# A retention block on one Trainium2 core: head outputs turned by four VectorE instructions a head, with the blocks put in place through DRAM

## The chip, the cores and the metric

The kernel runs on one core of one Trainium2 chip. Times are microseconds of device time. Matrix products run on TensorE (PE), elementwise work on VectorE (DVE) and ScalarE (ACT), small work and the software DMA queue on GpSimd (POOL), the hardware DMA queue on SyncE (SP). Each engine executes its own list of instructions strictly in order; semaphores join the lists. An instruction that waits holds everything behind it on its engine.

## The reference

One encoder layer on 512 tokens of width 1024, in float32:

```python
h = rmsnorm(x, g_mix);  proj = h @ w_in          # xc, gb, gc, q, k, v, g_sw, gate_a, gate_r
y_a = (gb * dwconv3(gc * xc)) @ w_a_out
ret = Ret_fwd(q, k, v) + Ret_bwd(q, k, v)        # 4 heads, q/k 256 wide, v 512 wide, rotary on q and k
ret = (ret - mean) * rsqrt(var + 1e-6)           # per token and head, over the 512 values
y_r = (ret * g_ret * silu(g_sw)) @ w_r_out       # 2048 x 1024
x = x + (sigmoid(gate_a) * y_a + sigmoid(gate_r) * y_r) @ w_o
x = x + (silu(h2 @ w_gate) * (h2 @ w_up)) @ w_down,  h2 = rmsnorm(x, g_ffn);  y = rmsnorm(x, g_final)
```

## The kernel before, in words

Every float32 operand is split into a high part in float32r and a low rest (`split`, L200: the high part on ACT at L203 or L206, the low part on DVE at L204 or L207), and each product is three matmuls, high by high, high by low, low by high (`mm3`, L340). Large products use a Strassen form (`strassen`, `fm_quad`). Weights come in pieces of 512 KB on the SP queue into a pool of 10 `raw` buffers, and are split into 5 pairs `whi`/`wlo` that are reused in turn.

The program first makes all projections. What is needed later is kept in DRAM: v and the silu of the gate, `sgd`, for each of the four heads (`do_quad`, L745, stores by `store`, L632, on the POOL queue), rotated q and k (`keep`), gates for the merge. Then comes the stage of the heads (L942 to L974):

- `load_head` brings q, k, v and the gate of the next head to SBUF on the SP queue.
- `do_scores` makes the 512 x 512 table of scores of a head, times its decay, 128 source tokens at a time (24 matmuls), and splits it into `p`.
- `do_pv` multiplies by v. For each tile `nb` of 128 tokens, 12 matmuls fill one PSUM bank with 128 tokens x 512 values; DVE takes mean and variance (L894 to L896), POOL the power (L897), DVE subtracts the mean and multiplies by the gate (L903), ACT scales (L905). The result lies in `sg`, tokens on partitions. At the last tile of a head, `sum_step` puts up to four DRAM transfers on the POOL queue (`t_o`), which add weight quarters for a later stage.
- `do_t` (L907) turns it: `transpose` (L212) issues 16 DVE instructions a head, each moving one quarter of 32 partitions to another, so that features lie on partitions. Then four `split`s with the gain `g_ret` make `yr`.
- `do_wr` multiplies `yr` by 512 rows of `w_r_out`, in two halves of 512 columns, each with four PSUM banks (96 matmuls in all), and adds to `ysum` (ACT copies at L935 for head 0, DVE adds at L937 for the others).

On PE the stage runs pv(0), scores(1), `do_mix(3)`, pv(1), scores(2), wr(0), pv(2), scores(3), wr(1), pv(3), wr(2), wr(3). So head h is turned after pv(h), and `yr` is first read one product later; for head 3 only wr(2) lies between. There are 8 PSUM banks (`psum`, L180) used in turn. A scheduler sets the order of each engine's list: it interleaves the instructions by its own forecast, and the order is then fixed.

Of the kernel before, what the change touches and what calls it, by code (L numbers as in the profile page):

```python
# [14 lines left out]
AF = mybir.ActivationFunctionType  # L15
ALU = mybir.AluOpType

P = 128
# [3 lines left out]
NB = S // P  # L22
HEADS = 4
# [148 lines left out]
def block_kernel(ctx: ExitStack, tc: tile.TileContext, xw0, xw, xT, xtok, wpack, wquad, cols, decs, rot, g_ffn, g_final, out):  # L172
    nc = tc.nc
# [26 lines left out]
    def split(src, hi, lo, scale=None, round=None):  # L200

        if scale is None:
            first = (round or nc.scalar.copy)(hi, src)  # L203
            low_of[0] = nc.vector.tensor_tensor(out=lo, in0=src, in1=hi.bitcast(F32), op=ALU.subtract)  # L204
        else:
            first = nc.scalar.activation(hi, src, AF.Copy, scale=scale)  # L206
            nc.vector.scalar_tensor_tensor(  # L207
                out=lo, in0=src, scalar=scale, in1=hi.bitcast(F32),
                op0=ALU.mult, op1=ALU.subtract)
        return first  # L210

    def transpose(out, src):  # L212

        for b in range(4):
            for q in range(4):
                i = src[32 * b:32 * b + 32].rearrange("p j (i q c) -> p j i q c", q=4, c=32)
                o = out[32 * q:32 * q + 32].rearrange("p i (j b c) -> p j i b c", b=4, c=32)
                nc.vector.transpose(o[:, :, :, b, :], i[:, :, :, q, :])


    pos = [0]
    block = [0]
# [42 lines left out]
    def sum_step(behind, among="quads"):  # L265

        if steps[among]:
            quad, f, g, u, add = steps[among].pop(0)
            src = wsum[quad, g, u] if g[0] == "t" else quarter(quad, g, u)
            with tc.issue_after(behind.ins):  # L270
                if add:
                    nc.gpsimd.dma_start(out=wsum[quad, f, u], in_=src, accum_op=ALU.add, max_dma_last_dim=4 * CH)
                else:
                    nc.gpsimd.dma_start(wsum[quad, f, u], src)
# [65 lines left out]
    def mm3(ps, left, right, first, last):  # L340
        (lh, ll), (rh, rl) = left, right
        nc.tensor.matmul(ps, lh, rh, start=first, stop=False)  # L342
        nc.tensor.matmul(ps, lh, rl, start=False, stop=False)  # L343
        nc.tensor.matmul(ps, ll, rh, start=False, stop=last)  # L344

    def act_pair(tiles, k, sl=slice(0, S)):
        hi, lo = tiles
        return hi[k // 4][:, k % 4, sl], lo[k // 4][:, k % 4, sl]
# [7 lines left out]
                mm3(ps, c.w(k, m * P, P), act_pair(rhs, k), k == 0, k == 7)  # L356
            evict(block0 + m, ps)

    def token_major(lhs, row0, chunks, evict, before=None):


        pss = [bank() for _ in range(NB)]
        n = 4 * chunks
        for kk in range(n):
            if kk % 4 == 0:
                c = Chunk()
            if before:
                before(kk)
# [117 lines left out]
    gret = cols_sb[:, O_GRET:O_GRET + 16]  # L486
# [109 lines left out]
    def decays():  # L596
        d = []
        for base, op in ((0, ALU.max), (-384, ALU.min)):
            delta = t512(mybir.dt.int32)
            nc.gpsimd.iota(delta, pattern=[[1, 512]], base=base, channel_multiplier=-1)  # L600
            d.append(t512())
            nc.vector.tensor_scalar(out=d[-1], in0=delta, scalar1=0.0, scalar2=None, op0=op)
        for h in range(HEADS):
            f, g = t512(), t512()
            nc.scalar.activation(f, d[0], AF.Exp, scale=lgam[:, h:h + 1])
            nc.scalar.activation(g, d[1], AF.Exp, scale=lgam[:, 4 + h:5 + h])
            nc.vector.tensor_tensor(out=f[:, 0:P], in0=f[:, 0:P], in1=g[:, 384:512], op=ALU.mult)
            store(tabs[h][:, 0:384], g[:, 0:384])
            store(tabs[h][:, 384:896], f)
# [3 lines left out]
    def kept(name):  # L613
        return dram.tile([P, 4, 512], F32, name=name)
# [17 lines left out]
    def store(dst, t):  # L632
        return nc.gpsimd.dma_start(dst, t)
# [4 lines left out]
    for h in range(EARLY):  # L638
        pss = [bank() for _ in range(4)]
        for kk in range(8):  # L640
            if kk % 4 == 0:
                c = Chunk()
# [23 lines left out]
        t = bigtile()  # L666
# [77 lines left out]

    def do_quad(left, right, func, func_left=None):  # L745
        def ev_sum(dst, o, f):
            def ev(tt, t):
                if f:
                    nc.scalar.activation(t, t, f)
                last = store(dst[:, o + tt, :], t)  # L750
                if tt and not o:
                    sum_step(last)
            return ev

        def ev21(tt, ps):
            t = t512()
            nc.scalar.activation(t, ps, func_left or AF.Copy)
            last = store(left[:, 2 + tt, :], t)
            if tt:
                turn_one()  # L760
                sum_step(last)
        strassen(4, xforms, ev_sum(left, 0, func_left), ev21, ev_sum(right, 2, func), ev_sum(right, 0, func))

    decays()
    for h in range(HEADS):
        do_quad(vd[h], sgd[h], AF.Silu)
        if h >= EARLY:
            do_qk(h)
    for j in range(2):
        do_quad(gad[j], grd[j], AF.Sigmoid, AF.Sigmoid)  # L770
    while held:
        turn_one()

# [89 lines left out]
    def do_scores(qk, tab):  # L863
        p = (bigtile(F32R), bigtile(F32R))
        for mb in range(NB):
            ps = bank()
            for d in range(2):
                sl = slice(mb * P, (mb + 1) * P)
                mm3(ps, (qk[0][:, 2 + d, sl], qk[1][:, 2 + d, sl]), (qk[0][:, d, :], qk[1][:, d, :]),
                    d == 0, d == 1)  # L870
            t = t512()
            o = (3 - mb) * P
            nc.vector.scalar_tensor_tensor(out=t, in0=ps, scalar=QK ** -0.5, in1=tab[:, o:o + 512],
                                           op0=ALU.mult, op1=ALU.mult)
            split(t, p[0][:, mb, :], p[1][:, mb, :])
        return p

    def split_v(v):
# [48 lines left out]
    def do_wr(h, yr):  # L927

        if h == 0:
            ysum.extend([bigtile(), bigtile()])  # L930
        for half in range(2):
            def ev(nb, ps):
                t = ysum[half][:, nb, :]
                if h == 0:
                    nc.scalar.copy(t, ps)  # L935
                else:
                    nc.vector.tensor_tensor(out=t, in0=ps, in1=t, op=ALU.add)  # L937
                if h == HEADS - 1:
                    nc.vector.tensor_tensor(out=t, in0=t, in1=sgr[half][:, nb, :], op=ALU.mult)
            token_major(yr, 0, 1, ev)  # L940

    mix_quads()  # L942
    nxt = load_head(0)
    p = do_scores(nxt[0], nxt[1])
    vv, sg = split_v(nxt[2]), nxt[3]
    do_mix(2)
    yr = None
    for h in range(HEADS):
# [5 lines left out]
        t = sg  # L954
        if h < HEADS - 1:
            p = do_scores(nxt[0], nxt[1])
# [10 lines left out]
        yr = new  # L967
# [107 lines left out]
    a, d, b = po["a"], [bank(), bank()], [bank(), bank()]  # L1075
# [227 lines left out]
    a, d, b = ([bank(), bank()] for _ in range(3))  # L1303
# [120 lines left out]
```

## Time and profile before

| what | value |
|---|---|
| median of 3 runs | 1022.72 us (1022.34 to 1023.39) |
| profiled execution, first to last instruction | 1021.7 us |
| PE busy | 1013.2 us (99%) |
| PE weight loads | 883.2 us (86%) |
| DVE busy | 902.5 us (88%) |
| ACT busy | 548.4 us (54%) |
| POOL busy | 151.7 us (15%) |
| HBM read and written | 162.8 MB and 57.4 MB |

The profile lists the profiled execution by its span alone; the three timed runs lie 0.6 to 1.7 us above that span. In the profile a line `L218` is a line of the source, the arrow `out<-in` names what an instruction writes and reads, and a square bracket in the timeline tells how long the engine had been idle before the instruction and what ended the wait. DMA landing times run from the issue to the arrival of the data.

### The profile page before, as it was taken

The numbers are of one execution on the slowest core, as the hardware profiler recorded it, in microseconds if no ns is written. First come the engines' busy times: TensorE is split into PE (matmuls) and PEld (weight loads), VectorE is DVE, ScalarE is ACT, GpSimd is POOL, SyncE is SP. The second block draws the span as 40 slices with busy tenths as digits, with TensorE's granted clock in tenths as the row PEclk, the third lists the DMA queues.
The fourth block names the chain that finished last, engine by engine and source line by source line (L and its number), as shares of the span: only waits on it lengthen the run. The fifth ranks groups of instructions, "written<-read, shape, count | busy, mean of one in ns | idle before, by whom it ended". The sixth has DMA issues, their size and how long they took to land.

```text
span 1021.7 us, 14821 instructions
## 1 busy us (share of the span) xinstructions
PE 1013.2 (99%) x5586; PEld 883.2 (86%) x5586; DVE 902.5 (88%) x1161; ACT 548.4 (54%) x744; POOL 151.7 (15%) x238
## 2 busy tenths in 40 slices
PE   9999999999999999999999999999999999999997
PEld 7888888888888998888888888889998999899986
DVE  7878998979798888797989997999898999889996
ACT  7547665553655455343543325586654565556554
POOL 0030221222122003202122100020001410110011
PEclk9999999999999999999999999999999999999999
DMA  9525587695767657839597855484316562663523
GB/s 354 188 81 185 173 296 212 214 310 162 249 196 238 250 203 268 333 130 349 124 331 294 272 200 169 157 264 132 107 42 242 172 154 83 198 153 104 165 69 98
DMA packets 53992, 202.34 MB, mean 198 GB/s; under 512 B 7392, under 2 KB 7520, under 8 KB 49312
## 3 DMA queue, kind: packets, MB, share of 16 engines
q1 hardware_dynamic: 37600, 137.39, 39.0%
q0 software_dynamic: 16032, 63.71, 21.3%
q8 instruction: 44, 0.72, 0.3%
q10 hardware_dynamic: 288, 0.29, 0.1%
q14 instruction: 28, 0.23, 0.1%
HBM read 162.82 MB, written 57.41 MB: 216 GB/s over the span
## 4 chain that ended last, share of the span: by engine, by line
PE 98%; DVE 1%; ACT 0%; issue 0%; POOL 0%; POOLq 0%; ACTq 0%
PE bank L427 39%; PE bank L383 27%; PE bank L342 10%; PE bank L343 10%; PE bank L344 10%; PE bank L477 0%; PE bank L1053 0%; PE bank L998 0%; PE bank L662 0%; DVE raw L301 0%; DVE big L1296 0%; ACT whi L203 0%; DVE wlo L204 0%; POOL fin L1286 0%; POOL ac L1035 0%
## 5 line engine op out<-in xcount | busy, mean ns | idle before, releaser
L203 ACT CAST whi<-raw 128x1024 fp32r<-128x1024 f32 (+2 forms) x299 | 302.8, 1028 | 265.0 <-PE bank L427 67.1
L204 DVE TENSOR_TENSOR wlo<-raw,whi 128x1024 fp32r<-128x1024 f32 (+2 forms) x300 | 352.7, 1192 | 68.0 <-ACT whi L203 67.7
L383 PE MATMUL bank<-xform,whi 128*128 128x256 f32 x1424 | 258.2, 284 | 0.3 <-ACT whi L203 0.3
L383 PEld LDWEIGHTS bank<-xform,whi 128*128 128x128 f32 x1424 | 222.3, 192 | 2.0 <-ACT t L434 0.8
L383 PE MATMUL bank<-xform,wlo 128*128 128x256 f32 x712 | 200.7, 283 | 0.0
L427 PE MATMUL bank<-whi,big 128*128 128x512 f32 x596 | 187.0, 389 | 0.0
L427 PE MATMUL bank<-whi,xform 128*128 128x512 f32 x496 | 157.1, 390 | 0.0
L301 DVE TENSOR_TENSOR raw<-raw 128x1024 f32<-128x1024 f32 (+1 forms) x128 | 152.0, 1203 | 4.2 <-DMA raw<-wquad 3.3
L383 PEld LDWEIGHTS bank<-xform,wlo 128*128 128x128 f32 x712 | 136.4, 192 | 0.0
L427 PEld LDWEIGHTS bank<-whi,big 128*128 128x128 f32 x596 | 111.9, 188 | 23.8 <-ACT t L434 0.4
L427 PE MATMUL bank<-wlo,big 128*128 128x512 f32 x298 | 115.7, 389 | 0.0
L427 PEld LDWEIGHTS bank<-whi,xform 128*128 128x128 f32 x496 | 93.0, 188 | 19.7 <-DVE xform L204 0.6
L427 PE MATMUL bank<-wlo,xform 128*128 128x512 f32 x248 | 96.5, 389 | 0.0
L434 ACT COPY t<-bank 128x512 f32<-128x512 f32 x105 | 61.0, 587 | 56.3 <-PE bank L383 30.1
L342 PE MATMUL bank<-big,whi 128*128 128x512 f32 x220 | 85.7, 390 | 0.0
L344 PE MATMUL bank<-big,wlo 128*128 128x512 f32 x220 | 85.6, 389 | 0.0
L343 PE MATMUL bank<-big,whi 128*128 128x512 f32 x220 | 85.6, 389 | 0.0
L427 PEld LDWEIGHTS bank<-wlo,big 128*128 128x128 f32 x298 | 56.0, 188 | 11.4
L427 PEld LDWEIGHTS bank<-wlo,xform 128*128 128x128 f32 x248 | 46.6, 188 | 9.6
L342 PE MATMUL bank<-whi,big 128*128 128x512 f32 x128 | 49.8, 389 | 0.0
L343 PE MATMUL bank<-wlo,big 128*128 128x512 f32 x128 | 49.8, 389 | 0.0
L344 PE MATMUL bank<-whi,big 128*128 128x512 f32 x128 | 49.8, 389 | 0.0
(203 smaller groups left out, 1385.8 us busy)
## 6 DMA issues: line engine op xcount, KB each, us to landing
raw<-wquad SPq DMA_DIRECT2D x140, 512.0 KB, 4.7
raw<-wpack SPq DMA_DIRECT2D x42, 512.0 KB, 6.3
t_f<-wquad POOLq DMA_DIRECT2D x12, 512.0 KB, 8.0
z<-t POOLq DMA_DIRECT2D x24, 256.0 KB, 4.5
t_o<-wquad POOLq DMA_DIRECT2D x12, 512.0 KB, 6.7
zform<-z POOLq DMA_DIRECT2D x6, 1024.0 KB, 7.8
v<-t POOLq DMA_DIRECT2D x16, 256.0 KB, 5.7
sg<-t POOLq DMA_DIRECT2D x16, 256.0 KB, 4.8
```

The costliest lines, as they stand in the source:

```text
L203: first = (round or nc.scalar.copy)(hi, src)
L204: low_of[0] = nc.vector.tensor_tensor(out=lo, in0=src, in1=hi.bitcast(F32), op=ALU.subtract)
L301: nc.vector.tensor_tensor(out=t, in0=t, in1=raws[quad, more, u][:, 0:n], op=ALU.add)
L342: nc.tensor.matmul(ps, lh, rh, start=first, stop=False)
L343: nc.tensor.matmul(ps, lh, rl, start=False, stop=False)
L344: nc.tensor.matmul(ps, ll, rh, start=False, stop=last)
L383: nc.tensor.matmul(o, l[:, c], r[:, k], start=start and s == 0 and k == 0 and i == 0, stop=stop and k == 3 and i == 2, skip_group_check=True)
L427: nc.tensor.matmul(pss[tt], l, r[:, c], start=start and k == 0 and i == 0, stop=stop and k == n - 1 and i == 2, skip_group_check=True)
L434: nc.scalar.copy(t, ps)
```

## The change

`transpose` now issues four DVE instructions a head, one for each token tile `j`, over all 128 partitions. Each turns blocks of 32 x 32 inside every quarter of 32 partitions and writes them in runs of 32 into a tile `t`. The blocks then go from one quarter of the partitions to another through DRAM: four stores on the POOL queue (256 KB each, by `store`) put them into a DRAM tensor `turned[h]`, and one load of 1 MB on the SP queue brings it back.

Tokens are assigned to tiles in another way: tile `j`, partition 32 b + r is token 128 b + 32 j + r. The split of the scores (L204 and L203 on `t`) writes its columns in that order, and the gate of a head is stored by quarters of 32 rows (`by_quarter`). The splits after turning read and write 4 runs of 128 for each partition instead of one run of 512. `token_major` loses arguments that were not used. The products are the same.

```diff
-    def transpose(out, src):
-
-        for b in range(4):
-            for q in range(4):
-                i = src[32 * b:32 * b + 32].rearrange("p j (i q c) -> p j i q c", q=4, c=32)
-                o = out[32 * q:32 * q + 32].rearrange("p i (j b c) -> p j i b c", b=4, c=32)
-                nc.vector.transpose(o[:, :, :, b, :], i[:, :, :, q, :])
+    def transpose(h, out, src):
+
+        t = bigtile()
+        for j in range(NB):
+            o = t.rearrange("p q (i j r) -> p i q j r", i=4, j=4)[:, :, :, j, :]
+            nc.vector.transpose(o, src[:, j, :].rearrange("p (i q c) -> p i q c", i=4, q=4))
+        for q in range(4):
+            store(turned[h][32 * q:32 * q + 32].rearrange("c b f -> b c f"), t[:, q, :])
+        nc.sync.dma_start(out, turned[h])
...
-    def token_major(lhs, row0, chunks, evict, before=None):
+    def token_major(lhs, evict):
...
-                mm3(pss[nb], act_pair(lhs, row0 + kk, slice(nb * P, (nb + 1) * P)),
-                    c.w(kk % 4, 0, 512), kk == 0, kk == n - 1)
+                mm3(pss[nb], tuple(x[:, nb, kk * P:(kk + 1) * P] for x in lhs), c.w(kk, 0, 512), kk == 0, kk == 3)
...
+    turned = [kept(f"turned{h}") for h in range(HEADS)]
...
-                last = store(dst[:, o + tt, :], t)
+                last = store(dst(o + tt), t)
...
+    def by_quarter(d):
+        return lambda n: d[32 * n:32 * n + 32].rearrange("r j e -> j r e")
...
-        do_quad(vd[h], sgd[h], AF.Silu)
+        do_quad(by_tile(vd[h]), by_quarter(sgd[h]), AF.Silu)
...
-            split(t, p[0][:, mb, :], p[1][:, mb, :])
+            split(t.rearrange("p (b j r) -> p b j r", b=4, j=4),
+                  *(x[:, mb, :].rearrange("p (j b r) -> p b j r", b=4, j=4) for x in p))
...
     def do_t(h, t):
         tt = bigtile()
-        transpose(tt, t)
+        transpose(h, tt, t)
         yr = (bigtile(F32R), bigtile(F32R))
         for eb in range(4):
-            split(tt[:, eb, :], yr[0][:, eb, :], yr[1][:, eb, :], gret[:, 4 * h + eb:4 * h + eb + 1])
-        return [yr[0]], [yr[1]]
+            split(*(x[:, :, P * eb:P * eb + P] for x in (tt, *yr)), gret[:, 4 * h + eb:4 * h + eb + 1])
+        return yr
```

The lists of the engines move with it. Line numbers of the changed kernel are 3 or 4 higher in this stage: L939 there is L935 here, L941 is L937, L630 is L633, L858 is L855.

**ACT, head 1 turned while wr(0) runs.** `L203 big<-t` is the end of the split of the scores of head 2, `L206` the high half of the split of the turned head 1, `L935` empties the banks of wr(0). Before:

```order
L203 CAST big<-t_4403 128x512
L203 CAST whi<-raw 128x1024 x2
L206 ACTIVATE big<-big,cols_sb 128x512 x4
L935 COPY big<-bank 128x512 x4
L203 CAST whi<-raw 128x1024
L935 COPY big<-bank 128x512 x4
```

And with the change:

```order
L203 CAST big<-t_4401 128x4x4x32
L203 CAST whi<-raw 128x1024 x3
L206 ACTIVATE big<-big,cols_sb 128x4x128 x4
L939 COPY big<-bank 128x512 x8
L203 CAST whi<-raw 128x1024
```

One cast of a weight moved ahead of the splits of head 1; all eight copies out of PSUM still stand behind them.

**POOL, head 3.** `L897` is the power of a token tile of pv(3), `L274` and `L272` copy and add weight quarters in DRAM, `L921` loads operands of the merge. Before:

```order
L897 TENSOR_TENSOR bnmv<-bnmv,mhalf 128x1
L274 DMA t_0_o<-t_0_o 16x8192
L274 DMA t_2_o<-t_2_o 16x8192
L272 DMA t_0_o<-wquad 64x2048
L272 DMA t_2_o<-wquad 64x2048
L921 DMA zform<-z_249 128x1024
```

And with the change:

```order
L901 TENSOR_TENSOR bnmv<-bnmv,mhalf 128x1
L275 DMA t_0_o<-t_0_o 16x8192
L275 DMA t_2_o<-t_2_o 16x8192
L925 DMA zform<-z_252 128x2048
L273 DMA t_0_o<-wquad 64x2048
L273 DMA t_2_o<-wquad 64x2048
L630 DMA turned_246<-big 4x32x512 x4
L925 DMA zform<-z_253 128x1024
```

The four stores of head 3 stand behind the two additions (`L273`), which wait for the two copies (`L275`) to land.

**SP, heads 2 and 3.** With the change, the loads of the turned heads stand among the loads of weights:

```order
L1264 DMA gf<-g_final 128x1024
L241 DMA raw<-wpack 128x1024
L220 DMA big<-turned_245 128x2048
L287 DMA raw<-wquad 128x1024 x5
L220 DMA big<-turned_246 128x2048
L287 DMA raw<-wquad 128x1024
L858 DMA big<-gr_241 128x2048
```

Before, the same loads of weights and gates stood there without the two of `turned`; the load of the gate `gr`, which the end of wr(3) multiplies by, came ahead of the last three of `wquad`.

More of the change, by code (lines that the diff above doesn't have):

```diff
@@ L357, in feature_major @@
             evict(block0 + m, ps)
-    def token_major(lhs, row0, chunks, evict, before=None):
+    def token_major(lhs, evict):
         pss = [bank() for _ in range(NB)]
[L363 to L368, printed above, removed]
+        c = Chunk()
+        for kk in range(4):
             for nb in range(NB):
-                mm3(pss[nb], act_pair(lhs, row0 + kk, slice(nb * P, (nb + 1) * P)),
-                    c.w(kk % 4, 0, 512), kk == 0, kk == n - 1)
+                mm3(pss[nb], tuple(x[:, nb, kk * P:(kk + 1) * P] for x in lhs), c.w(kk, 0, 512), kk == 0, kk == 3)
         for nb in range(NB):
@@ L757, in ev21 @@
             nc.scalar.activation(t, ps, func_left or AF.Copy)
-            last = store(left[:, 2 + tt, :], t)
+            last = store(left(2 + tt), t)
             if tt:
@@ L769, in block_kernel @@
     for j in range(2):
-        do_quad(gad[j], grd[j], AF.Sigmoid, AF.Sigmoid)
+        do_quad(by_tile(gad[j]), by_tile(grd[j]), AF.Sigmoid, AF.Sigmoid)
     while held:
@@ L939, in ev @@
                     nc.vector.tensor_tensor(out=t, in0=t, in1=sgr[half][:, nb, :], op=ALU.mult)
-            token_major(yr, 0, 1, ev)
+            token_major(yr, ev)
     mix_quads()
```

2 lines of the change are left out of this document (added).

## The prediction

> **What bounds the kernel now.** I read the page first, then who waits for whom on PE, then the timelines of the engines around the places where a turned head is read.
>
> ```profile
> span 1021.7 us, 14821 instructions
> PE 1013.2 (99%) x5586; PEld 883.2 (86%) x5586; DVE 902.5 (88%) x1161; ACT 548.4 (54%) x744; POOL 151.7 (15%) x238
> PE 98%; DVE 1%; ACT 0%; issue 0%; POOL 0%; POOLq 0%; ACTq 0%
> ...
> PE bank L477 <- DVE t L474: 1.4, 1, 1.4
> PE bank L1053 <- DVE t L1039: 0.5, 1, 0.5
> PE bank L383 <- ACT whi L203: 0.3, 1, 0.3
> ```
>
> PE is busy in 1013.2 of 1021.7 us, 98% of the chain that ended last is PE, and PE's waits on other engines add up to 2.2 us, none in the stage of the heads. So PE sets the time, and the change leaves PE the same matmuls. Less work on DVE can then give next to nothing; the question is only whether something that PE reads, or a bank that it writes, comes later than now. PE reaches the two places that matter here at these times:
>
> ```profile
> 509.41 0.39 PE L344 MATMUL bank<-whi,big 128*128 128x512 f32 x1
> 509.63 0.39 PE L342 MATMUL bank<-big 128*128 128x512 f32 x1
> ...
> 580.13 0.39 PE L344 MATMUL bank<-whi,big 128*128 128x512 f32 x1
> 580.35 0.39 PE L342 MATMUL bank<-whi,big 128*128 128x512 f32 x1
> ```
>
> At 509.63 wr(0) is over and pv(2) starts; at 580.35 wr(2) is over and wr(3) starts, the first reader of turned head 3. A matmul starts every 0.23 us without a gap.
>
> **Removed from DVE.** The transposes:
>
> ```profile
> L218 DVE STREAM_TRANSPOSE big<-big x64: 693/703/708, 443.0 to 572.2; 32x512 f32<-32x512 f32 x64
> ...
> L204 DVE TENSOR_TENSOR big<-t,big 128x512 fp32r<-128x512 f32 x12 | 8.0, 686 | 0.2 <-ACT big L203 0.2
> ...
> 493.45 11.45 DVE L218 STREAM_TRANSPOSE big<-big 32x512 f32<-32x512 f32 x16
> 530.07 11.44 DVE L218 STREAM_TRANSPOSE big<-big 32x512 f32<-32x512 f32 x16
> 561.47 11.45 DVE L218 STREAM_TRANSPOSE big<-big 32x512 f32<-32x512 f32 x16 [0.85 <-ACT big L905]
> ```
>
> The first row gives the shortest, median and longest of the 64, and the first and last start. A transpose of 512 elements on 32 partitions takes 703 ns. One over 128 partitions is not in the trace. Its bounds are the same 0.70 us, if the four quarters run side by side, and 4 x 0.70 = 2.8 us, if the time goes by elements. I take 0.70, since a subtraction of 512 elements on all 128 partitions takes 686 ns. [...] So a head is turned in 4 x 0.715 = 2.9 us (11.45 / 16 apiece in the row), 8.6 us sooner than now, and DVE does 48 x 0.703 = 33.7 us less. On PE's path that is worth 0. The other edits to forms (writes of the scores in runs of 32, splits over 4 x 128, gate stores by quarters) keep elements per partition and the 2 KB pieces; I take 0 for them, at most some 0.1 us apiece beside PE.
>
> **Added: a way through DRAM.** After the fourth transpose POOL issues four stores, all have to land, SP issues a load of 1 MB, that has to land, and only then come the splits on ACT and DVE. Prices:
>
> ```profile
> L633 POOL DMA_DIRECT2D sg<-t x16: 542/542/566, 103.3 to 231.9; - x16
> DMA to landing us min/median/max: 2.4/4.1/9.8
> ...
> L855 SPq DMA_DIRECT2D big<-qh x4: 326/327/331, 336.0 to 510.5; - x4
> DMA to landing us min/median/max: 5.5/8.7/14.6
> ...
> big<-gr SPq DMA_DIRECT2D x2, 1024.0 KB, 6.7
> ```
>
> Stores of this size cost POOL 0.54 to 0.69 us each (0.69 is the median of another form of store) and land after 2.4 to 9.8 us, loads of 1 MB after 5.5 to 14.6; a load with little beside it, as `gr`, after 6.7. Stores issued one behind the other add some 0.6 us apiece, so the last leaves 1.9 us after the first.
>
> Heads 0 and 2 have room. Head 0 is turned at 443.0 + 2.9 = 445.9; with the slowest store and the load's median, 445.9 + 1.9 + 9.8 + 8.7, it is back at 466.3, and wr(0) starts 96 matmuls, 21.7 us, ahead of 509.6, at 487.9. Head 2 is back by 530.1 + 2.9 + 1.9 + 9.8 + 8.7 = 553.4 at such prices, and its reader wr(2) starts at 580.35 - 21.7 = 558.6.
>
> **First stall: head 1.** The head is turned at 493.45 + 2.9 = 496.3, but what stands behind it on ACT is urgent:
>
> ```profile
> 504.94 2.56 ACT L206 ACTIVATE big<-big,cols_sb 128x512 fp32r<-128x512 f32 x4 [4.93 <-DVE big L218]
> 507.41 2.02 ACT L935 COPY big<-bank 128x512 f32<-128x512 f32 x4
> ...
> 486.20 3.29 POOL L272 DMA_DIRECT2D t_o<-wquad  x4
> ...
> GB/s 406 418 426 397 217 0 0 66 82 229 188 246 188 205 238 213 274 254 270 184 8 0 0 0 0 0 0 164 336 25 12 180 258 369 418 426 418 418 426 442
> ```
>
> The four splits `L206` wait for the turned head, 2.47 us later the copies `L935` begin, which empty the banks of wr(0). Both halves of wr(0) hold four banks each, all eight, so pv(2) can't start at 509.63 until the first copy is done. Today that is at 507.41 + 0.5 = 507.9, 1.7 us in time. With the change the order of ACT still has all copies behind the splits. The stores go out from 496.3 to 498.3. POOL's four additions `t_o`, issued at 486.2, are ahead of them in its queue; the last row, what the DMA engines moved in each microsecond from 480 to 520, shows them moving until 500 and then nothing until 507. At the 426 GB/s of busy slices 1 MB takes 2.5 us, so the stores land near 503.7, a little over a microsecond after the last byte; the load, some 6.2 us (between 5.5 and 6.7), at 510. First copy done at 510 + 2.47 + 0.5 = 513.0: PE stands 3.4 us. Low end: 498.3 + 2.4 + 5.5 + 3.0 = 509.2, no stall. High end: 498.3 + 9.8 + 8.7 + 3.0 = 519.8, a stall of 10.2.
>
> **Second stall: head 3.** Only wr(2) lies between its pv and its reader. In POOL's list the stores come behind two additions, and these wait for two copies in DRAM:
>
> ```profile
> 560.64 1.03 POOL L274 DMA_DIRECT2D t_o<-t_o  x2
> 567.94 0.84 POOL L272 DMA_DIRECT2D t_o<-wquad  x1 [6.27 <-DMA t_o<-t_o]
> 569.16 0.78 POOL L272 DMA_DIRECT2D t_o<-wquad  x1 [0.38 <-DMA t_o<-t_o]
> ...
> GB/s 421 279 350 317 426 426 197 426 350 262 0 0 76 98 175 197 240 186 197 186 131 208 360 448 382 339 393 399 333 366 202 273 300 344 333 317 355 415 426 410
> ...
> 569.72 1.05 ACT L203 CAST whi<-raw 128x1024 fp32r<-128x1024 f32 x1 [4.39 <-PE bank L344]
> 572.96 2.57 ACT L206 ACTIVATE big<-big,cols_sb 128x512 fp32r<-128x512 f32 x4 [2.19 <-DVE big L218]
> ...
> 572.95 1.29 DVE L937 TENSOR_TENSOR big<-bank,big 128x512 f32<-128x512 f32 x2
> ...
> 578.00 1.22 DVE L204 TENSOR_TENSOR wlo<-raw,whi 128x1024 fp32r<-128x1024 f32 x1
> ```
>
> The head is turned at 561.5 + 2.9 = 564.4, the 8.6 us won are lost here: the stores can't go out before 569.9, the last at 571.8. The additions ahead of them move at some 200 GB/s from 569 to 575 (the row has 0.75 us a number, from 560), so the stores land near 577.4; 4.1 alone would give 575.9. SP is free then: the weight loads ahead of the turned head wait for a `wlo` whose cast ends at 570.8, and with four adds (4 x 0.64) and the split itself (1.22) ahead on DVE that is over by 574. Load at 577.6, landed 583.8, first split 0.64 later (2.57 / 4), 584.4; PE wants it at 580.35, so it stands 4.1 us. Low end: 571.8 + 2.4 + 5.5 + 0.64 = 580.3, no stall; high end: 571.8 + 9.8 + 8.7 + 0.64 = 590.9, a stall of 10.6. Head 2's splits, later than now, stand ahead of pv(3)'s statistics on DVE; as an allowance without a row I add 0.5: 4.6 us. Behind the load on SP queue one piece of weights for the merge stage and the two `gr`, which wr(3) reads only at the end of its first half, 10.9 us after its start.
>
> **Sum.** 3.4 + 4.6 = 8.0 us. PE has no later slack to win it back, and all that follows moves along. 1021.7 + 8.0 is a span of 1029.7; the median of the runs lies 1.0 above the span, so **1030.7 us**.
>
> **The rivals.**
>
> *The trips fit.* Both low ends above come out at no stall. For it: from 500 to 507 the DMA engines are empty, so the load of head 1 would run alone. Against it: the shortest landing of all stores and the shortest of all loads of those lines would have to fall together, at both places. Then the time is 1022.7, with at most 0.5 us from a less busy DVE. [...] Chance 0.10.
>
> *One of the two stalls only.* The load of head 1 lands alone on empty engines below 507 (then 1022.7 + 4.6 = 1027.3), or head 3's stores pass the additions in the queue (then 1022.7 + 3.4 = 1026.1). Chance 0.14, 1027.
>
> *Transposes by elements.* A turn stays at 11.45 us, and the trip starts where the turn ends now: head 1 at 504.9 + 1.9 + 4.1 + 6.2 + 3.0 = 520.1, a stall of 10.5; head 3 at 572.9 + 1.9 + 4.1 + 6.2 + 0.6 = 585.7, a stall of 5.4. Sum 15.9, 1038.6. Against it the lane rate of the subtraction above. Chance 0.06.
>
> **How the numbers follow.** Both stalls: 0.70, 1030.7, by itself 1026 to 1036, since each can miss by some 3 us either way. With the single stall below and most of the slow ends above, 8 in 10 lie in 1025 to 1037. About 0.2% (2 us) is what a measurement of this kernel can tell from no change. Slower: 0.70 + 0.14 + 0.06 = 0.90. The fit splits into 0.07 same and 0.03 faster.
>
> **What would show it.** PE idle in the changed profile, with a wait of pv(2)'s first matmul on ACT's L939 (about 3.4 us) and one of wr(3)'s first on ACT's L206 (about 4.6 us), both absent now. ACT waiting on a DMA into `big` from `turned` at L206. Transposes at 0.70 us x16. Stores of head 3 issued after L273's additions. Wrong would be: no PE wait there; transposes near 2.8 us; a stall at wr(1) or wr(2), which I rule out; or the whole trip, last transpose to landed load, under 9 us or over 22.

## The result, and the profile after

The changed kernel takes 1072.1 us (median of 4 runs, 1068.05 to 1077.05), beside 1023.1 of the kernel before on the same chip: 1.048 times as long, 95% interval 1.045 to 1.051. The forecast was 1030.7, with 1025 to 1037 as its range. The direction was right, the size six times too small: the profiled execution grew by 48.0 us where 8.0 were summed. Of all executions in this document one, of best_a, was slow throughout (1267 us at a granted clock of 0.75) and is left out of every figure.

First the page of the changed kernel, then who waits for whom on PE (us in total, times, longest):

```profile
span 1069.7 us, 14807 instructions
PE 1019.7 (95%) x5586; PEld 885.3 (83%) x5586; DVE 869.0 (81%) x1113; ACT 547.7 (51%) x744; POOL 163.9 (15%) x254
DMA packets 61992, 210.78 MB, mean 197 GB/s; under 512 B 13856, under 2 KB 13984, under 8 KB 56800
...
PE bank L343 <- ACT big L206: 22.1, 1, 22.1
PE bank L343 <- ACT big L939: 13.8, 1, 13.8
PE bank L343 <- DVE big L907: 2.9, 4, 0.8
PE bank L422 <- ACT t L429: 1.6, 1, 1.6
```

The two waits that the prediction named are there, on the lines that it named, L939 at head 1 and L206 at head 3; but they are 13.8 and 22.1 us instead of 3.4 and 4.6. The waits on L907, in the stage of the heads, and on L429, in the projections, were not in it. DVE is relieved as computed, 902.5 - 869.0 = 33.5 us, and PE has nothing of it.

Busy time by stretch shows a further loss. The columns after the stretch are its length, the busy times of PE, PE's weight loads, DVE, ACT and POOL, the granted PE clock, the share of the DMA engines and GB/s:

```profile
515.90:529.80 13.90, 0.08 (x1) 0.00 (x0) 2.29 (x4) 3.05 (x6) 0.04 (x1) 0.68 0.57 192
529.80:534.50 4.70, 4.67 (x11) 3.71 (x12) 0.44 (x1) 4.32 (x8) 0.00 (x0) 0.50 1.01 425
...
625.30:630.00 4.70, 4.63 (x11) 3.67 (x12) 4.58 (x6) 2.79 (x5) 0.53 (x1) 0.50 1.00 408
```

After each long wait PE runs for 4.7 us at half the clock: 11 matmuls take 4.7 us, at 0.23 us a start it would be 2.5, so 2.2 us are lost each time. Compared matmul by matmul, the changed kernel lags 2.1 us behind the one before at 258 us, 6.1 when the first four banks of wr(0) are open, 22.5 after head 1's stall, 47.4 after head 3's, and 47.7 at the end: nothing is won back, as predicted.

Now the trips. POOL's timeline at heads 1 and 3 (`L630` issues the stores), and for each the landing (shortest, median, longest) of its first store alone:

```profile
506.11 2.12 POOL L630 DMA_DIRECT2D turned<-big  x3 [6.91 <-DVE big L217]
515.27 0.67 POOL L630 DMA_DIRECT2D turned<-big  x1 [7.03 <-issue]
...
598.16 0.84 POOL L273 DMA_DIRECT2D t_o<-wquad  x1 [5.25 <-DMA t_o<-t_o]
599.15 0.79 POOL L273 DMA_DIRECT2D t_o<-wquad  x1 [0.15 <-issue]
599.69 2.32 POOL L630 DMA_DIRECT2D turned<-big  x3
611.55 0.68 POOL L630 DMA_DIRECT2D turned<-big  x1 [9.53 <-issue]
...
DMA to landing us min/median/max: 8.8/8.8/8.8
...
DMA to landing us min/median/max: 11.5/11.5/11.5
```

Three stores go out, then POOL stands 7.0 and 9.5 us, and the fourth goes 0.4 us after the first has landed (506.11 + 8.8 = 514.9 and 599.69 + 11.5 = 611.2); no instruction of the list stands between. The same holds at heads 0 and 2. By the timelines the whole trips, last transpose to landed load, take 22.2, 21.1, 21.7 and 30.9 us at heads 0 to 3, where the prediction had 20.4 at most at heads 0 and 2, 13.7 at head 1 and 19.4 at head 3. The load is not what is slow (5.0 us, with 6.2 reckoned); the stores are, and the gates' stores, which have the same form now (median landing of the kernel before: 4.8):

```profile
turned<-big POOLq DMA_DIRECT2D x16, 256.0 KB, 8.9
big<-turned SPq DMA_DIRECT2D x4, 1024.0 KB, 5.0
sg<-t POOLq DMA_DIRECT2D x16, 256.0 KB, 7.7
```

The page also counts 13856 packets under 512 bytes, 7392 before. Their sizes in the trace: on the software queue 6144 of 8 bytes, 192 for each of the 32 stores whose destination is 4 x 32 x 512; the kernel before has none.

### The profile page after: what moved, and what is told of

It is laid out like the page before. It is cut to its first block, busy times and chain, and to the rows that moved or that the text cites. A ratio compares the mean times of both kernels' runs of the same rounds, so it can differ in the third digit from the quotient of the medians.

```text
span 1069.7 us, 14807 instructions
## 1 busy us (share of the span) xinstructions
PE 1019.7 (95%) x5586; PEld 885.3 (83%) x5586; DVE 869.0 (81%) x1113; ACT 547.7 (51%) x744; POOL 163.9 (15%) x254
## 2 busy tenths in 40 slices
DMA packets 61992, 210.78 MB, mean 197 GB/s; under 512 B 13856, under 2 KB 13984, under 8 KB 56800
## 5 line engine op out<-in xcount | busy, mean ns | idle before, releaser
L203 ACT CAST whi<-raw 128x1024 fp32r<-128x1024 f32 (+2 forms) x299 | 302.6, 1028 | 252.3 <-PE bank L422 62.6
L204 DVE TENSOR_TENSOR wlo<-raw,whi 128x1024 fp32r<-128x1024 f32 (+2 forms) x300 | 353.0, 1192 | 79.4 <-ACT whi L203 78.7
L422 PE MATMUL bank<-whi,big 128*128 128x512 f32 x596 | 187.0, 389 | 0.0
L422 PE MATMUL bank<-wlo,big 128*128 128x512 f32 x298 | 115.7, 389 | 0.0
L429 ACT COPY t<-bank 128x512 f32<-128x512 f32 x105 | 60.8, 585 | 56.3 <-PE bank L378 30.1
L343 PE MATMUL bank<-big,whi 128*128 128x512 f32 x220 | 85.7, 390 | 0.0
L343 PE MATMUL bank<-whi,big 128*128 128x512 f32 x128 | 51.4, 402 | 25.0 <-ACT big L206 22.1
L207 DVE SCALAR_TENSOR_TENSOR big<-big,cols_sb 128x512 fp32r<-128x512 f32 x16 | 11.0, 748 | 58.8 <-ACT big L206 58.8
L422 PEld LDWEIGHTS bank<-wlo,xform 128*128 128x128 f32 x248 | 46.6, 188 | 10.7 <-DVE wlo L204 1.3
L343 PE MATMUL bank<-big 128*128 128x512 f32 x96 | 38.5, 401 | 13.8 <-ACT big L939 13.8
```

The costliest lines, as they stand in the source:

```text
L207: nc.vector.scalar_tensor_tensor(out=lo, in0=src, scalar=scale, in1=hi.bitcast(F32), op0=ALU.mult, op1=ALU.subtract)
L422: nc.tensor.matmul(pss[tt], l, r[:, c], start=start and k == 0 and i == 0, stop=stop and k == n - 1 and i == 2, skip_group_check=True)
```

## The experiments

Times are medians; ratios are to the kernel before, run beside each group (1022.8 to 1023.5). Diffs are against the changed kernel where nothing else is said.

### Is it the trip? no_trip

```diff
-        t = bigtile()
+        t = out
...
-        for q in range(4):
-            store(turned[h][32 * q:32 * q + 32].rearrange("c b f -> b c f"), t[:, q, :])
-        nc.sync.dma_start(out, turned[h])
```

> The splits read the tile that the four transposes wrote; no stores, no load, so the blocks stay in their quarters (the exchange of quarters is left out). Theory F and the prediction agree that all of the stage's loss is the trip: 1023 to 1027 us, what is left of the loss being the gates' 2 us, and no wait of PE over 1 us at L206 or L939. Rival: the writes in runs of 32 and the splits in runs of 128 cost DVE and ACT time that PE waits for; then 1030 us or more, with waits of PE on DVE or ACT left in the stage of the heads.

Measured: 1030.6 us, ratio 1.0064 (1.0042 to 1.0086). More than expected, but not where the rival had it. PE's waits:

```profile
PE bank L422 <- ACT t L429: 2.5, 1, 2.5
PE bank L422 <- DVE wlo L204: 2.3, 2, 1.8
```

L343, the stage of the heads, is gone from the list. So the transposes, the splits in runs of 32 and those in runs of 128 cost PE nothing there, and 41 of the 49 us are the trip. What is left lies mostly in the projections, where the gates are stored (below): matmul by matmul the run lags 6.5 us there and 1.1 more behind the heads.

### The form of the turned stores: plain_store

```diff
-            store(turned[h][32 * q:32 * q + 32].rearrange("c b f -> b c f"), t[:, q, :])
+            store(turned[h][32 * q:32 * q + 32].rearrange("c b f -> (c b) f"), t[:, q, :])
```

> The four stores of a turned head go row by row to 128 successive rows of DRAM instead of by blocks to 4 x 32 rows; the load, all queues and the order on every engine stay as in the change, so the blocks come back in the wrong quarters (that part of the computation is left out). Theory F (the form of the store is what was mis-sized: with the permuted destination a store of 256 KB landed in 6.4 to 11.5 us, and the fourth was issued 0.4 us after the first had landed, never sooner): the four go out in 4 x 0.55 = 2.2 us, the last lands some 4 to 6 us later, each trip is about 10 us shorter. PE's wait at head 1 falls from 13.8 to about 4, at head 3 from 22.1 to 4 to 10, the 2.9 us at L907 go, the slow matmuls behind the waits become fewer: 1034 to 1046 us. Rival W (the way itself, behind what POOL has queued and through loaded DMA engines, whatever the form): the waits stay within 3 us of 13.8 and 22.1, 1066 to 1074 us.

Measured: 1046.9 us, ratio 1.0232 (1.0206 to 1.0258), 25 us less than the change and 0.9 above what was expected. PE's waits, and POOL's stores of head 1:

```profile
PE bank L343 <- ACT big L206: 9.8, 1, 9.8
PE bank L343 <- ACT big L939: 4.2, 1, 4.2
...
501.71 2.21 POOL L630 DMA_DIRECT2D turned<-big  x4 [6.71 <-DVE big L217]
```

Four in a row, none held. The order is the same on every engine, so the form alone is worth 25 us, half of the loss. At this point I held the packets of 8 bytes for the reason.

### Packets or engines: sp_store

```diff
-            store(turned[h][32 * q:32 * q + 32].rearrange("c b f -> b c f"), t[:, q, :])
+            nc.sync.dma_start(turned[h][32 * q:32 * q + 32].rearrange("c b f -> b c f"), t[:, q, :])
```

> As the change, but SP's hardware queue issues the four stores of a turned head, in the same permuted form. Theory F1 (the packets of 8 bytes are made only where the software queue of POOL carries such a form): the turned stores bring none, so under 512 B falls from 13856 to about 10800, they land in 2 to 6 us, and the time is 1040 to 1055 us, the rest being SP, which now waits for the transposes with weights behind it. Theory F2 (the form itself makes them, on any queue): 13800 small packets again, landing over 7 us, 1062 us or more.

Measured: 1070.6 us, ratio 1.0461 (1.0445 to 1.0477). Each theory has one half wrong: the packets of 8 bytes of the turned stores are gone (10592 under 512 bytes), and the time is that of the change. SP's timeline at head 0, then the DMA of four microseconds in which only these stores move; below it three microseconds of plain_store's stores of head 0, on POOL:

```profile
448.56 3.07 SPq L219 DMA_DIRECT2D turned<-big  x4
451.99 2.25 SPq L241 DMA_DIRECT2D raw<-wpack  x1
462.71 0.33 SPq L220 DMA_DIRECT2D big<-turned  x1
...
DMA packets 205, 0.41 MB, mean 102 GB/s; under 512 B 5, under 2 KB 5, under 8 KB 205
q1 hardware_dynamic: 205, 0.41, 26.3%
```

```profile
DMA packets 295, 1.01 MB, mean 336 GB/s; under 512 B 49, under 2 KB 49, under 8 KB 295
q0 software_dynamic: 295, 1.01, 90.4%
```

26.3% of 16 engines is what four of them, busy all the time, would show (4.2), though four stores had been issued one behind the other; 1 MB at 102 GB/s takes 10.3 us, and the load goes out 11.1 us after the last store. The plain form used 90.4% of them at 336 GB/s. The destination, 4 x 32 x 512, begins with a 4. That gave theory E.

### Engines or scattered rows: four_blocks, outer_32, eight_blocks

```diff
# four_blocks (eight_blocks with b=8)
-            store(turned[h][32 * q:32 * q + 32].rearrange("c b f -> b c f"), t[:, q, :])
+            store(turned[h].rearrange("(b q k) j f -> q b (k j) f", b=4, q=4)[q], t[:, q, :])
# outer_32
-        for q in range(4):
-            store(turned[h][32 * q:32 * q + 32].rearrange("c b f -> b c f"), t[:, q, :])
+        for b in range(4):
+            store(turned[h][:, b, :].rearrange("(q c) f -> c q f", q=4), t[32 * b:32 * b + 32])
```

> As the change, order and form (4x32x512) on every engine the same, but each of the four runs of 32 rows in the destination of a turned store lies in a row in DRAM, 64 KB apiece (the blocks come back in the wrong places: the exchange is left out). Theory E, formed on sp_store (1 MB of stores without a packet of 8 bytes ran at 104 GB/s with four packets in flight, where plain stores had 16 and 380 GB/s): a destination that begins with a dimension of 4 is carried by 4 of the 16 DMA engines, wherever the rows lie. Then nothing changes: 1066 to 1077 us, waits near 14 and 22. Theory S (the rows of 2 KB at a stride of 8 KB are what is slow): 1040 to 1052 us, waits near 4 and 10.

> The whole computation: the four stores of a turned head take one quarter of 32 partitions each, all four pieces of every partition, to the same addresses in the same rows of 2 KB as in the change, so their destination is 32x4x512 instead of 4x32x512; the load of 1 MB stays. Theory E: all 16 engines carry them, some 250 to 400 GB/s, landing 3 to 7 us when little else moves, waits of PE near 4 and 10 us, 1042 to 1053 us, even if packets of 8 bytes stay. Theory S: landing over 8 us, 1064 us or more. Rival B (the packets of 8 bytes and the fourth store held until the first has landed are the price on POOL): 1060 us or more if the packets are there.

> As four_blocks, but the destination of a turned store is 8 blocks of 16 rows (8x16x512, each block in a row in DRAM; the exchange is left out), order on every engine the same as in the change. Theory E by degree: 8 of 16 engines, some 210 GB/s, so the stores land between those of four_blocks (7 to 11 us) and plain_store (2.4 to 11 us), and the time lies between 1046.9 and 1073.7: 1050 to 1063 us, waits of PE of 6 to 10 and 12 to 18 us. Rival (anything but a plain 128x512 costs the same, whatever its first dimension): 1066 us or more.

Measured: four_blocks 1073.7 us, ratio 1.0489 (1.0472 to 1.0505); outer_32 1053.4, 1.0296 (1.0283 to 1.0309); eight_blocks 1053.0, 1.0293 (1.0261 to 1.0325). PE's waits in four_blocks, in outer_32 and in eight_blocks, each in this order:

```profile
PE bank L343 <- ACT big L206: 21.2, 1, 21.2
PE bank L343 <- ACT big L939: 14.1, 1, 14.1
```

```profile
PE bank L343 <- ACT big L206: 14.0, 1, 14.0
PE bank L343 <- ACT big L939: 8.9, 1, 8.9
...
L630 POOL DMA_DIRECT2D turned<-big x4: 552/565/586, 447.0 to 448.7; - x4
DMA to landing us min/median/max: 3.0/4.3/4.7
```

```profile
PE bank L343 <- ACT big L206: 14.5, 1, 14.5
PE bank L343 <- ACT big L939: 5.8, 1, 5.8
```

The two landing lines are those of outer_32's stores of head 0. From the first issue to the last landing of the four stores, in us, by the timelines and landings:

| run | destination | head 0 | head 1 | head 2 | head 3 |
|---|---|---|---|---|---|
| the change | 4x32x512 | 16.5 | 15.6 | 16.1 | 19.6 |
| four_blocks | 4x32x512 | 14.6 | 15.7 | 16.1 | 18.9 |
| eight_blocks | 8x16x512 | 10.2 | 8.8 | 11.3 | 12.2 |
| outer_32 | 32x4x512 | 6.4 | 12.8 | 8.0 | 14.0 |
| plain_store | 128x512 | 4.8 | 8.6 | 7.8 | 12.8 |

Blocks of 64 KB in a row are as slow as scattered rows as long as the destination begins with 4; with 8 ahead the time of the program lies between; and outer_32's scattered rows, the same as the change's, go with 32 ahead almost as fast as plain rows at heads 0 and 2. So here it is the first dimension. The order on every engine is that of the change in four_blocks, eight_blocks and plain_store. For outer_32 the scheduler chose another one: SP puts more weights ahead of the load, which at head 0 goes out at 462.0 though the stores are there by 453.4, and 1.84 MB of weights beside the stores of head 1, 0.92 in plain_store. So its heads 1 and 3 and its time, which also missed the upper end of its expectation by 0.4 us, are no clean comparison.

The rate of sp_store is not the whole price on POOL. At head 0 little else moves (0.52 MB), and 1 MB at the 102 GB/s of sp_store takes 10.3 us; with the 1.7 us that plain_store's 4.8 has above 1 MB at 336 GB/s an estimate is 12.0, where the change takes 16.5. Only with a leading 4 on POOL was the fourth store held until the first had landed (four_blocks holds it too, eight_blocks does not), and only there came 192 packets of 8 bytes a store (64 in eight_blocks). What these packets are, and why the store is held, stays open.

### The gates: gates_by_tile

```diff
-        do_quad(by_tile(vd[h]), by_quarter(sgd[h]), AF.Silu)
+        do_quad(by_tile(vd[h]), by_tile(sgd[h]), AF.Silu)
```

> Only the stores of the four gates go back to their old form, 128 rows in a row (each gate row then multiplies another token: the permutation of the gate is left out); order on every engine the same as in the change. Theory F: PE's lag of about 2 us at 230 to 260 us, where banks wait for ACT's L429 and for wlo, goes: 1.5 to 3 us faster than the change, and the landing of the gate stores falls from 7.7 us to about 5. Rival (the lag comes from the new forms of other work): within 1 us of the change.

Measured: 1068.1 us, ratio 1.0438 (1.0423 to 1.0453), 4 us less than the change and more than the 1.5 to 3 expected (single executions of the two overlap: 1066.5 to 1069.5, and 1068.1 to 1077.1); the median landing of the gate stores falls from 7.7 to 4.2 us. Busy time from 225 to 262 us, of the change and of gates_by_tile:

```profile
225.00:262.00 37.00, 35.42 (x156) 28.99 (x155) 32.13 (x40) 13.98 (x18) 8.30 (x14) 1.00 0.60 180
```

```profile
225.00:262.00 37.00, 37.00 (x165) 30.65 (x164) 33.79 (x42) 15.56 (x20) 7.32 (x13) 1.00 0.59 180
```

PE is without a gap again, as in the kernel before. The stores of the gates in quarters land later, and the buffers that they read come free later; that this is what delays ACT's and DVE's buffers is read from who waits for whom (DVE waits 5.4 us for these stores in the change, not at all in gates_by_tile). The size varies: at 300 us the ten runs with stores in quarters, the change among them, lag 1.2 (outer_32) to 8.9 us (eight_blocks) behind the kernel before, the six with gates stored to 128 rows under 0.6 us either way.

### The order on ACT: split_late

```diff
     def do_t(h, t):
         tt = bigtile()
         transpose(h, tt, t)
+        return tt
+
+    def split_t(h, tt):
         yr = (bigtile(F32R), bigtile(F32R))
...
             do_wr(h - 1, yr)
-        yr = new
+        yr = split_t(h, new)
```

> Transposes, stores and load of a head stay where they are in the code, its four splits come behind the product wr of the head before it, so ACT empties wr(0)'s banks (L939) ahead of them, and do_mix(3) is no longer behind head 0's splits. Theory F, with the places as seen: the wait of 13.8 us of pv(2) on L939 and the 2.9 us on L907 go, with some 2 us of slow matmuls; the trips themselves stay at 20 us and more and head 3's wait stays within 5 us of 22: 1050 to 1057 us. Rival (the stall only moves on: the later splits hold up wr(1) or the statistics of pv(2) instead): 1062 us or more, with a new wait of over 8 us before wr(1) or pv(3).

Measured: 1065.3 us, ratio 1.0414 (1.0388 to 1.044). The time is the rival's, its sign is not: no new wait of over 8 us came. L939 is gone from PE's waits, the wait of head 3 on L206 stays, and smaller ones came:

```profile
PE bank L343 <- ACT big L206: 23.9, 1, 23.9
...
PE bank L343 <- DMA big<-qh: 3.5, 1, 3.5
PE bank L344 <- DMA big<-ql: 1.6, 1, 1.6
```

The load of head 1 waits on SP until the slow stores have landed, and PE waits 3.5 and 1.6 us for the next head's q and k, which stand behind it in SP's list. So the order of the splits alone is worth 6.8 us here, where the wait on L939 was 13.8.

### POOL's queue, and the sum: adds_behind, order_kept, copies_first

```diff
# adds_behind, against plain_store
-            if nb == NB - 1:
+            if nb == NB - 1 and add:            # add: not for head 3
...
                 sgr = [load(t) for t in grd]
+                for _ in range(4):
+                    sum_step(stored[0], "heads")    # stored[0]: the last turned store
# order_kept, against adds_behind
-        do_quad(by_tile(vd[h]), by_quarter(sgd[h]), AF.Silu)
+        do_quad(by_tile(vd[h]), by_tile(sgd[h]), AF.Silu)
# copies_first, against order_kept: split_late's edit for heads 0 and 1 alone
```

> As plain_store (1046.9 us, waits 4.2 and 9.8; the exchange of quarters is again wrong in the data alone), and in addition the four transfers t_o of head 3 stand behind the turned stores in POOL's list instead of ahead of them. Theory Q (what is left of head 3's wait is POOL's queue and the traffic of t_o, as the prediction's second stall has it): the stores go out some 7 us sooner against PE and land in 3 to 7 instead of 10.6 to 11.1 us; PE's wait on L206 falls from 9.8 to under 3 us, 1033 to 1040 us, if the sums t_o, now later, are still in time for their readers. Rival (the wait is the trip's own length): still above 7 us, 1043 us or more.

> adds_behind (plain turned stores, t_o of head 3 behind them) with the gates stored by tile as in gates_by_tile; the permutation of the gates and the exchange of quarters are left out, the order is the one of adds_behind on every engine. If the three causes add up: 1035.8 less the gates' 3 to 5 us, 1030 to 1033.5 us, with no lag of PE at 230 to 260 us, a wait of about 4 us on L939 and 2.3 us of slow matmuls behind it as all that is left. Rival (they overlap, or the trip holds up something else): 1035 us or more.

> order_kept with the splits of heads 0 and 1 behind the product wr (and do_mix(3)) that follows them in the code, so that ACT empties wr(0)'s banks ahead of head 1's splits. If the trip has no price of its own once its form, POOL's queue and ACT's order are out: no wait of PE over 1.5 us in the stage of the heads, 1023 to 1027.5 us, at most 0.4% above the kernel before. Rival (the trip itself cannot be hidden): one wait of 4 us or more stays, 1029 us or more.

Measured: adds_behind 1035.8 us, ratio 1.0127 (1.0113 to 1.0142); order_kept 1031.0, 1.0077 (1.0062 to 1.0092); copies_first 1024.4, 1.0008 (0.9998 to 1.0017). The stores of head 3 in plain_store and in adds_behind, and PE's wait in the stage of the heads that is left in copies_first:

```profile
L630 POOL DMA_DIRECT2D turned<-big x4: 726/748/837, 581.0 to 582.7; - x4
DMA to landing us min/median/max: 10.6/10.9/11.1
```

```profile
L630 POOL DMA_DIRECT2D turned<-big x4: 539/544/558, 574.1 to 575.7; - x4
DMA to landing us min/median/max: 5.9/6.8/7.5
```

```profile
PE bank L343 <- ACT big L206: 1.4, 1, 1.4
```

All three came out as expected. Ahead of `t_o` the stores go out 7 us sooner and land 4 us faster, and the wait at head 3 falls from 9.8 to 0.9 us. With all four causes out the program has the trip and the 16 transposes, and cannot be told from the kernel before; but the three runs leave out the exchange of quarters, and the last two the permutation of the gates as well. So the loss adds up, from 1072.1 down, each step in this order: form of the turned stores 25.2, POOL's queue at head 3 11.1, gates 4.8, ACT's order at head 1 6.6 (4.1 of wait and its slow matmuls), left over 1.1 above the 1023.4 beside it.

### The whole computation in other forms: load_puts, all_plain, best_a, best_b

```diff
# load_puts
+        rows = [turned[h][32 * q:32 * q + 32].rearrange("k j f -> (k j) f") for q in range(4)]
         for q in range(4):
-            store(turned[h][32 * q:32 * q + 32].rearrange("c b f -> b c f"), t[:, q, :])
-        nc.sync.dma_start(out, turned[h])
+            store(rows[q], t[:, q, :])
+        for q in range(4):
+            nc.sync.dma_start(out[32 * q:32 * q + 32], rows[q].rearrange("(b c) f -> c b f", b=4))
# all_plain: load_puts, the same for the gates (four loads 32x4x512 a head), adds_behind's edit
# best_a: all_plain with outer_32's stores and one load; best_b: best_a with split_late's edit
```

> The whole computation, with plain stores of 128 rows and the blocks put in place by the load, four loads of 32 x 4 x 512 on SP for each head instead of one of 1 MB. Theory F: as plain_store, 1042 to 1052 us, waits near 4 and 10, no packets of 8 bytes for the turned heads. Rival (a permutation costs the same on whichever side it stands): the loads land in over 9 us, the waits stay over 10 and 18 us, 1060 us or more.

> The whole computation, with load_puts' way for the turned heads and for the gates too (plain stores, four permuting loads), and head 3's t_o transfers behind its stores. If form and queue position are all that the change costs beyond head 1's stall: no lag of PE at 230 to 260 us, wait at head 3 under 3 us, wait at head 1 about 4 us and its 2.3 us of slow matmuls: 1027 to 1036 us. Rival (the trip by itself holds up more, at the gates' loads or at head 3): 1040 us or more.

> The whole computation: outer_32's stores, gates stored in plain rows and loaded in four pieces as in all_plain, t_o of head 3 behind the turned stores. Theories E and Q together leave head 1's wait of some 4 us, its slow matmuls of 2.3 us, and under 3 us at head 3: 1026 to 1034 us. If 1038 us or more, the trip has a price beyond form and queue.

> best_a with the splits of a head behind the product wr of the head before it, so that ACT empties wr(0)'s banks ahead of head 1's splits. Head 1's wait goes too: 1022 to 1028 us, level with the kernel before, since PE had no wait to lose there. Rival, as split_late showed it: the turned load on SP holds up the next head's q and k, a wait of 3 to 5 us at scores; then 1028 to 1036 us.

Measured: load_puts 1051.1 us, ratio 1.0273 (1.0254 to 1.0291); all_plain 1041.6, 1.0186 (1.0162 to 1.0211); best_a 1047.9, 1.0235 (1.0219 to 1.0250); best_b 1037.2, 1.0135 (1.0121 to 1.0148). The first is within its expectation, 4.2 us above plain_store: at heads 1 and 3 the last of its four loads lands 5.1 and 5.0 us after the last store, in plain_store the one load 5.1 and 7.5. At head 2, where PE has time, it is 10.1 and 5.3. So a permutation on the load's side, with 32 ahead, is not free, but does not bring the price of the leading 4. The other three missed theirs by 6 to 14 us: all_plain and best_a come out where their expectations give the trip a price of its own, best_b above its rival too, and without that rival's wait at scores. The lag at the gates is gone in all three, but the scheduler laid the stage out anew in each: against PE the stores of head 3 go out 5.0, 7.4 and 10.4 us later in all_plain, best_a and best_b than in adds_behind. In all_plain the last of the four loads of head 3 also lands 9.2 us after the last store, where adds_behind has 7.1. In best_b the turn of head 3 stands on DVE behind the adds of wr(2):

```profile
568.00 2.73 DVE L943 TENSOR_TENSOR big<-bank,big 128x512 f32<-128x512 f32 x4 [1.10 <-PE bank L345]
...
572.31 2.48 DVE L217 STREAM_TRANSPOSE big<-big 128x512 f32<-128x512 f32 x4
```

The head's values are ready some 10 us earlier (ACT's last L909 ends at 562.3), and PE waits 10.7 us for it. None of the complete versions reaches the kernel before. One in copies_first's order was not built, so whether the whole computation can have the trip for nothing is not shown.

## Why the prediction was right or wrong

**PE sets the time, and DVE's relief is worth nothing**: right. 33.5 us less on DVE, none of it on PE; and each microsecond lost in the stage stays lost to the end.

**The transposes** at 0.70 us: right, and the rival by elements is out.

```profile
L217 DVE STREAM_TRANSPOSE big<-big x16: 668/670/705, 445.2 to 593.0; 128x512 f32<-128x512 f32 x16
```

**"The other edits to forms ... I take 0 for them"**: a first term that was put at nothing and was not. It holds for the splits (no_trip), but among these edits were the gate stores by quarters, which cost 4.0 and 4.8 us in the two pairs of runs. "Keep the 2 KB pieces" was true and did not matter.

**"Prices"**: the step that failed, by its size. The landing times of 2.4, 4.1 and 9.8 us are those of all 120 stores at L633 of the kernel before, none of which begins with 4; the new stores have another form, and their own landing is 6.4 to 11.5 us, with the fourth held back. The diff gives both forms, `dst[:, o + tt, :]` with 128 rows ahead and `c b f -> b c f` with 4, and should have stopped me. No row of the prediction shows the second form, so its size was not to be had there. As an estimate from sp_store's 102 GB/s, 1 MB takes 10.3 us where I had 2.5, and the first stall becomes some 11 us (3.4 + 7.8). So what was mis-sized is the landing of the stores, by their form; on POOL the held fourth store came on top.

**First stall**: place and releaser right. In the true form 13.8 us; with the form that the price was taken from 4.2, beside 3.4. The mechanism stands. That the two are so close is in part luck: less the lag, plain_store's stores landed at 505.8, where I had 503.7 (with an allowance of a microsecond after the last byte that stands on no row), and its load took 5.0 us instead of 6.2.

**Second stall**: place and releaser right, 22.1 us; 9.8 with the plain form. There the stores went out as reckoned (569.2 less the lag, 569.9 reckoned), but beside `t_o` they landed after 10.6 to 11.1 us, where I had 5.6 for the last, and the load took 7.4 instead of 6.2. In the changed kernel they also went out 7 us later against PE than reckoned: 599.69, less the lag of 22.5, is 577.2, and I had 569.9. The reason is in the sentence "as an allowance without a row I add 0.5": head 2's splits stand on DVE ahead of pv(3)'s statistics,

```profile
577.74 2.74 DVE L207 SCALAR_TENSOR_TENSOR big<-big,cols_sb 128x512 fp32r<-128x512 f32 x4 [10.40 <-ACT big L206]
...
583.92 0.69 DVE L898 BATCH_NORM_STATS2 bnst<-bank 128x6 f32<-128x512 f32 x1
```

and with the statistics the powers on POOL, the two copies and two additions of `t_o` behind them, and the turn of head 3 all move. Less the lag, the first statistics are at 561.4, at 552.4 in the kernel before: 9 us, not 0.5. Head 2 was back at 554.3 less the lag, beside the 553.4 that the prediction itself had with the slowest store; the splits of head 2, four adds and a low half of weights, ahead of the statistics on DVE, take it from there. (A smaller slip: 570.8, four adds and the split make 574.6, not 574; nothing hangs on it.)

**"Heads 0 and 2 have room"**: their readers on PE did not wait, but what stood behind their splits did. Head 0's splits, late, stand ahead of `do_mix(3)` on ACT and DVE, whose last split then waits for the stores `z`, and pv(1)'s statistics come behind it:

```profile
489.55 0.43 DVE L204 TENSOR_TENSOR t<-big,t 128x256 fp32r<-128x256 f32 x1 [2.89 <-DMA z<-t]
...
489.96 0.74 DVE L907 SCALAR_TENSOR_TENSOR big<-bank,bnmv,big 128x512 f32<-128x512 f32 x1
...
490.84 0.47 PE L343 MATMUL bank<-whi,big 128*128 128x512 f32 x1 [0.61 <-DVE big L907]
```

That is a stall at wr(0) of 2.9 us, which the prediction did not look for. It went with the form (plain_store has none).

**Left out altogether**: the slow matmuls behind a long wait, 2.2 us for each, 4.4 in all.

**The sum** of the traced loss, with 2.1 us of lag at the gates: 22.1 + 13.8 + 2.9 + 4.4 + 2.1 is 45.3 of 48.0; the rest is not placed.

**The rivals.** "The trips fit" is reached by copies_first, with other stores, another order and a part of the computation left out; the change as it stands is far from it. "One of the two stalls only" is out, both came. Of the signs of being wrong, "the whole trip over 22 us" came true at heads 0 and 3.

## What to carry to other kernels

Price a DMA by a row of the same form, above all the same first dimension: here four stores whose destination begins with 4 kept 26.3% of the 16 engines busy at 102 GB/s on the hardware queue, where plain ones on the software queue had 90.4% and 336, and took 16.5 us instead of 4.8 on the software queue at head 0; with 8 or 32 ahead it was 10.2 and 6.4. Where a transfer makes something late, follow the lists of the engines behind the late instruction as far as the next turn of the loop; here what stood behind a split put the next head's trip off by 7 us. In this kernel, where PE is busy for 99% of the time, 33.5 us less on DVE gained nothing, and the waits of 13.8 and 22.1 us cost PE another 2.2 us each.

## What the runs showed of the hardware

- Four stores of 256 KB to 4 x 32 x 512, issued one behind the other on SP, ran at 26.3% of 16 engines and 102 GB/s; stores to 128 rows from POOL at 90.4% and 336.
- On POOL such a store brought 192 packets of 8 bytes (64 with 8 ahead, none with 32 or in the plain form), its issue took 0.71 instead of 0.57 us, and the fourth was not issued before the first had landed, in 4 of 4 heads. Four of them took 16.5 us at head 0, in the plain form 4.8. Why was not tried.
- After PE had waited 13.8 and 22.1 us the granted clock was 0.50 for 4.7 us and a matmul started every 0.43 instead of 0.23 us; after the 4.2 us of plain_store it was the same for 5.9 us, after the 4.1 of adds_behind for about 3.3.
